# Attention stages of a two-layer backbone: end of the gate chain and its transposes issued behind the mLSTM key and query projections, convolution mean as a later step

## The chip, the core and the metric

The kernel runs on one core of a Trainium2 chip. The engines of a core work side by side and meet at semaphores: TensorE (PE) multiplies matrices, VectorE (DVE) and ScalarE (ACT) work element by element, GpSimd (POOL) does simple element-wise work, and SyncE (SP) issues the DMA transfers in the order of its own queue. The metric is the device time of one execution in microseconds (us), lower is better.

## The reference, cut to what matters

Two layers over 512 tokens of width 1024 (256 context tokens, 256 latent tokens; layer 1 needs the latent ones alone as outputs). Each layer has an attention stage and an expert stage:

```python
u  = adaLN_rmsnorm(x)                  # scale and shift come from c @ ada_w
a, q, k, v, o, gates, dq, dk, dv = split(u @ in_w)
# 1. conv module: gated input, depthwise convolution over 31 taps, layernorm, silu
y  = silu(layernorm(depthwise_conv31(a1 * sigmoid(a2)) + conv_b))
# 2. bidirectional mLSTM, 4 heads of 64: input and forget gates per head and direction
F  = cumsum(log_sigmoid(fgate));  M = running_max(igate - F)
w  = exp(igate - F - M) * (q @ k.T)    # masked on one side per direction
h1 = (w @ v) / max(|sum(w)|, exp(-(F + M)))
# 3. differential attention, 4 heads, rotary positions
h2 = (softmax(q1 @ k1.T) - lam * softmax(q2 @ k2.T)) @ dv
x += gate * (concat(y, h1, h2) @ out_w)
x += gate * peer_experts(adaLN_rmsnorm(x))   # product keys, 16384 experts
```

## The kernel before

The kernel is one program, written once in a natural order. A scheduler sets each engine's instruction order from that program and from a model of the work; where two instructions meet in one buffer, a semaphore makes the later one wait. Buffers are tiles of a pool with a **tag**: tiles with one tag share the tag's slots, and a new tile waits until the slot's former tile has been read for the last time.

An attention stage (`front`) runs as follows, at 50 to 345 us of the span in layer 0 and 2057 to 2300 us in layer 1:

- **Projections.** `proj` and `projv` read weights of 512 KB each on SP's queue; ACT writes the high part of each weight (`whi`), POOL the rest (`wlo`), and PE makes 24 matmuls for each projection (lines 319 to 321, three products per weight block; `projv` lines 350 to 352). The order in the program is: gate rows and conv inputs (`projg`, lines 333 to 335), second conv input, mLSTM output gates (MO0, MO1), mLSTM keys (MK0, MK1), queries (MQ0, MQ1), values, and then the steps of the string `ORDER`.
- **Gate chain.** `gate_rows` works on tiles of 64 rows x 512 tokens (heads and directions in rows): from line 520 to line 561 some 40 small operations of DVE with a few of ACT between them, scans included (lines 547 and 551). Its last part takes an exp, writes `rows` (line 565), and turns the chain's columns with eight transposes on PE (line 571) into `ah` and `ea`, which the heads need.
- **Convolution.** `conv` makes 62 multiply-adds on DVE (2 blocks x 31 taps, line 491 for 60 of them), then the layernorm: a mean by two matmuls on PE (line 495), line 497, squares, an rsqrt, lines 503 and 504, and a sigmoid on ACT (line 507).
- **mLSTM heads.** For each head PE spreads `rows` (line 613), ACT and DVE write the decay matrix E (lines 621, 625, 627), PE multiplies queries by keys (line 634), DVE multiplies that into E (line 639), and PE makes E times values (line 645).
- **Late modulation, layer 0 only.** `late` computes three of the six adaLN vectors. Its weights come as 12 tiles `w` of 1 MB, which use the slots of tags `kT` and `qT` in turn. PE multiplies half the columns of a tile (line 216) and DVE the other half (lines 147 and 149, four operations a tile), into an accumulator tile of tag `PT`, which has two slots.

The string `ORDER` is 'kmcvkk0k123' before: k is one pair of rotary keys and queries, m the mLSTM heads, c the whole convolution, v the values, digits are heads of differential attention.

Of the kernel before, what the change touches and what calls it, by code (L numbers as in the profile page):

```python
# [7 lines left out]
F32 = mybir.dt.float32  # L8
# [4 lines left out]
AF = mybir.ActivationFunctionType  # L13
# [22 lines left out]
LO = ('p', 'p')  # L36
ORDER = ('kmcvkk0k123', 'kmcvkk0k123')
NSUM = 4
# [11 lines left out]
class Net:  # L50
# [317 lines left out]
    def front(self, l, P, c0, late):  # L368
# [17 lines left out]
        first = self.projg(I["w_first"][l, 0], h, 0, ("f", "f", "f", "d"))  # L386
        rows = self.gate_rows(P, first[0], K)

# [6 lines left out]
        og = K["og"] = F.tile([128, 2, n], F32, name="og")  # L395
        v = K["v"] = F.tile([128, 4, 512], F32, name="v", tag="v")
        up = F.tile([128, 2, ns, T + 30], F32, name="up")
# [17 lines left out]
        for b in range(2):  # L415
            nc.scalar.activation(mq[:, b], self.proj(W[BLK_MQ + b], h, c0), AF.Copy)
        for k, p in enumerate(self.projv(I["w_v"][l, 0], h)):
            pv = p.rearrange("p t (a b e) -> p t a b e", b=2, e=64)
            for tt in range(2):
                for b in range(2):  # L420
                    nc.scalar.activation(vx[:, 2 * k + tt, b::2, 64 * b:64 * b + 64], pv[:, tt, :, b, :], AF.Copy)
# [11 lines left out]

        def values():
            for k in range(2):
                for t2, p in enumerate(self.projv(I["w_v"][l, 1 + k], h)):
                    nc.scalar.activation(v[:, 2 * t2:2 * t2 + 2, 256 * k:256 * k + 256], p, AF.Copy)
# [3 lines left out]
        for s in ORDER[l]:  # L441
            if s == "m":
                self.mlstm(P, K, rows, c0)
            elif s == "c":
                cy = self.conv(P, up, n)
            elif s == "v":
                values()
            elif s == "k":
                keys(seen)
                seen += 1  # L450
            else:
                self.diff(P, K, int(s), c0)
# [30 lines left out]
    def conv(self, P, up, n):  # L483
        nc = self.nc
        ys = [self.frontp.tile([128, n], F32, name=f"cy{b}") for b in range(2)]
        for b in range(2):
# [3 lines left out]
            for k in range(1, CONV_K):  # L490
                nc.vector.scalar_tensor_tensor(y, up[:, b, :, k:k + T], P["conv_w"][:, b, k:k + 1], y,  # L491
                                         op0=OP.mult, op1=OP.add)
        mu = self.ps("a")[:, :n]
        for b in range(2):
            nc.tensor.matmul(mu, self.ones, ys[b], start=b == 0, stop=b == 1)
        for b in range(2):
# [12 lines left out]
        self.log_exp(last)  # L509
        return ys  # L510

    def gate_rows(self, P, ps, K):

        nc, F = self.nc, self.frontp
        T1 = F.tile([128, 4, TT], F32, name="gr1", tag="v")
        T2 = F.tile([64, 4, TT], F32, name="gr2", tag="vx")
        G = T1[:, 0]
        Fg, e, u = (T1[0:64, k] for k in (1, 2, 3))
        r, L, Bl, M = (T2[:, k] for k in range(4))
        nc.vector.tensor_scalar(G, ps, P["gate_b"][:, 0:1], None, op0=OP.add)  # L520
# [11 lines left out]
        nc.vector.scalar_tensor_tensor(L, Fg, 0.0, L, op0=OP.min, op1=OP.subtract)  # L532
        lh, ll, ih, il = e, u, r, Fg

# [26 lines left out]
        nc.vector.tensor_add(out[:, 1], out[:, 1], Bl)  # L561
        nc.scalar.activation(out[:, 1], out[:, 1], AF.Exp, scale=-1.0)
        rows = F.tile([128, 2, TT], F32R, name="rows")
# [5 lines left out]
        for k, src in enumerate((ih, il)):  # L569
            for tt in range(4):  # L570
                nc.tensor.transpose(pt[:, (4 * k + tt) * 64:(4 * k + tt) * 64 + 64],
                                    src[:, tt * 128:(tt + 1) * 128], self.ident[:64, :64])
        pv = pt.rearrange("p (k t r) -> p k t r", k=2, t=4)
# [612 lines left out]
```

## Time and profile before

| quantity | before |
|---|---|
| time, median of 3 runs | 3119.13 us (3117.34 to 3130.06) |
| the profiled execution: time, span | 3119.87 us, 3118.2 us |
| TensorE's granted clock over the span | 0.973 of full speed |
| PE busy | 2933.3 us, 94% of the span |
| DVE busy | 2233.9 us, 72% |
| ACT, POOL busy | 1440.0 us, 1378.2 us |

Busy times are shares of the whole span, while the change touches two stretches of some 290 and 240 us. What bounds those has to be read from windows of the trace, from the list of waits and from the timeline of each engine in them.

### The profile page before, as it was taken

How to read it: one execution, taken by the hardware profiler on the slowest of the kernel's cores; microseconds unless marked ns; L12 is line 12 of the kernel's file. 1: busy time of each engine (PE TensorE's matmuls, PEld its weight loads, DVE VectorE, ACT ScalarE, POOL GpSimd, SP SyncE). 2: the span in 40 equal slices, each digit the busy share in tenths (PEclk: the TensorE clock that was granted, in tenths of full speed). 3: DMA queues.
4: the chain of work that ended last, by engine and by line, in shares of the span. 5: the costliest groups of instructions: out<-in, count | busy, mean ns of one | idle time of the engine just before them, and what ended most of it. 6: DMA issues, size and time to landing. Idle time of an engine off the chain costs nothing.

```text
span 3118.2 us, 43562 instructions
## 1 busy us (share of the span) xinstructions
PE 2933.3 (94%) x14930; PEld 2424.5 (78%) x14930; DVE 2233.9 (72%) x4604; ACT 1440.0 (46%) x2861; POOL 1378.2 (44%) x1079
## 2 busy tenths in 40 slices
PE   7899989999999978989999999978989998999998
PEld 4476578888888856767888888867689998788887
DVE  7987637867777769998555545486759789666665
ACT  4345443346666632223333333345455765555554
POOL 4434245656666645343434334163478875000000
PEclk9999999999999989999999999989999999999999
DMA  6511124345655577776555555121255876987874
GB/s 225 176 48 55 39 82 137 123 146 182 209 207 208 208 237 254 239 239 213 174 174 169 179 154 180 41 87 51 67 172 170 274 257 234 314 267 256 260 229 136
DMA packets 249806, 550.95 MB, mean 177 GB/s; under 512 B 17440, under 2 KB 118304, under 8 KB 246384
## 3 DMA queue, kind: packets, MB, share of 16 engines
q1 hardware_dynamic: 248864, 545.74, 53.3%
q8 instruction: 118, 1.93, 0.3%
q0 software_dynamic: 720, 2.43, 0.2%
q14 instruction: 104, 0.85, 0.1%
HBM read 456.87 MB, written 91.23 MB: 176 GB/s over the span
## 4 chain that ended last, share of the span: by engine, by line
PE 64%; DVE 13%; DMA 5%; issue 2%; ACT 1%; POOL 1%; SPq 0%; DVEq 0%; ACTq 0%; POOLq 0%
PE h L887 9%; PE h L888 9%; PE h L889 9%; PE acc L1000 6%; PE acc L999 5%; PE acc L1001 5%; PE f L836 3%; DVE wtr L196 3%; PE f L999 3%; PE f L1000 3%; PE f L1001 3%; DMA ga<-act 1%; DMA v<-in_peer_v 1%; DVE cy L491 1%; DMA u<-in_peer_u 1%
## 5 line engine op out<-in xcount | busy, mean ns | idle before, releaser
L870 POOL TENSOR_TENSOR ul<-u,uh 128x512 fp32r<-128x512 f32 x448 | 594.8, 1339 | 382.9 <-ACT uh L869 370.5
L887 PE MATMUL h<-hh,uh 128*128 128x512 f32 (+1 forms) x2048 | 694.4, 339 | 3.2 <-DVE rt_stg L838 2.1
L889 PE MATMUL h<-hh,ul 128*128 128x512 f32 (+1 forms) x2048 | 691.2, 338 | 5.1 <-POOL ul L870 5.1
L888 PE MATMUL h<-hl,uh 128*128 128x512 f32 (+1 forms) x2048 | 691.5, 338 | 0.0
L869 ACT ACTIVATE vh<-v 128x512 fp32r<-128x512 f32 x512 | 319.5, 628 | 590.1 <-PE acc L1001 368.3
L869 ACT ACTIVATE uh<-u 128x512 fp32r<-128x512 f32 x512 | 318.4, 628 | 468.2 <-PE h L888 320.8
L870 POOL TENSOR_TENSOR vl<-v,vh 128x512 fp32r<-128x512 f32 x208 | 303.3, 1470 | 366.5 <-ACT vh L869 357.3
L889 PEld LDWEIGHTS h<-hh,ul 128*128 128x128 f32 x2048 | 391.0, 191 | 46.7 <-POOL ul L870 5.8
L887 PEld LDWEIGHTS h<-hh,uh 128*128 128x128 f32 x2048 | 391.3, 191 | 45.4 <-DVE rt_stg L838 2.7
L888 PEld LDWEIGHTS h<-hl,uh 128*128 128x128 f32 x2048 | 391.4, 191 | 38.0
L1000 PE MATMUL acc<-vl,wh 128*128 128x512 f32 x1024 | 402.5, 393 | 4.3 <-DVE vl L870 4.1
L999 PE MATMUL acc<-vh,wh 128*128 128x512 f32 x1024 | 401.6, 392 | 1.5 <-ACT vh L869 1.5
L1001 PE MATMUL acc<-vh,wl 128*128 128x512 f32 x1024 | 400.6, 391 | 0.0
L241 POOL TENSOR_TENSOR wlo<-wt,whi 128x512 fp32r<-128x512 f32 x164 | 248.1, 1524 | 246.4 <-ACT whi L240 224.5
L838 DVE TENSOR_REDUCE rt_stg<-f 128x256 f32<-128x512 f32 x384 | 243.6, 687 | 137.4 <-PE f L836 136.6
L965 DVE TENSOR_TENSOR ga<-ga,g 128x512 f32<-128x512 f32 x192 | 163.2, 856 | 177.4 <-DMA ga<-act 99.6
L870 DVE TENSOR_TENSOR vl<-v,vh 128x512 fp32r<-128x512 f32 x304 | 205.6, 693 | 107.4 <-ACT vh L869 107.1
L999 PE MATMUL f<-vh,wh 128*128 128x512 f32 x512 | 205.1, 401 | 44.8 <-DVE accS L1007 34.3
L1000 PEld LDWEIGHTS acc<-vl,wh 128*128 128x128 f32 x1024 | 193.7, 189 | 49.2 <-DVE vl L870 9.2
L1007 DVE TENSOR_TENSOR accS<-accS,f 128x512 f32<-128x512 f32 x252 | 171.3, 680 | 83.0 <-PE f L1001 82.9
L999 PEld LDWEIGHTS acc<-vh,wh 128*128 128x128 f32 x1024 | 193.9, 189 | 42.5 <-ACT vh L869 2.2
L1001 PEld LDWEIGHTS acc<-vh,wl 128*128 128x128 f32 x1024 | 193.6, 189 | 40.2
(320 smaller groups left out, 5372.1 us busy)
## 6 DMA issues: line engine op xcount, KB each, us to landing
u<-in_peer_u SPq DMA_DIRECT2D x256, 512.0 KB, 4.1
v<-in_peer_v SPq DMA_DIRECT2D x256, 512.0 KB, 4.4
G<-rt_stg SPq DMA_DIRECT2D x24, 2048.0 KB, 7.0
act<-ga SPq DMA_DIRECT2D x152, 256.0 KB, 3.4
ga<-act SPq DMA_DIRECT2D x152, 256.0 KB, 4.2
g<-G SPq DMA_DIRECT2D x32, 1024.0 KB, 6.2
wa<-in_ada_t SPq DMA_DIRECT2D x56, 512.0 KB, 4.2
w<-in_ada_w SPq DMA_DIRECT2D x20, 1024.0 KB, 6.4
```

The source lines that it names most:

```text
L241: nc.gpsimd.tensor_sub(lo, raw, hi)
L838: nc.vector.tensor_reduce(stg[:, :, t4 + k2:t4 + k2 + 2].rearrange("p j t -> p t j"), pg.rearrange("p (t x j) -> p t j x", t=2, x=2), axis ...
L869: nc.scalar.activation(hi, raw[:, k * 512:(k + 1) * 512], AF.Copy)
L870: lo_eng.tensor_sub(lo, raw[:, k * 512:(k + 1) * 512], hi)
L887: nc.tensor.matmul(o, uh, hh[:, c, c0:], start=c == 0, stop=False)
L888: nc.tensor.matmul(o, uh, hl[:, c, c0:], start=False, stop=False)
L889: nc.tensor.matmul(o, ul, hh[:, c, c0:], start=False, stop=c == NB - 1)
L965: nc.vector.tensor_mul(av, av, g)
L999: nc.tensor.matmul(A, wh[:, t], vh, start=s0 and jj == 0, stop=False)
L1000: nc.tensor.matmul(A, wh[:, t], vl, start=False, stop=False)
L1001: nc.tensor.matmul(A, wl[:, t], vh, start=False, stop=s1 and jj == 1)
L1007: nc.vector.tensor_add(o, o, A)
```

## The change

Three things change, in both layers. First, `gate_rows` ends at line 561, and its last part (exp, `rows`, transposes, `ah`, `ea`) becomes `gate_cols`, called behind the key and query projections; its exp and its transposes are held in program order. Second, buffers: the four temporary rows that were one tile of tag `vx` are now two tiles `gr2` and `gr3` of tag `PT`, and the tiles `v` and `vx` get their slots in other places. Third, `conv` ends with the taps, and the layernorm with sigmoid becomes a step n that stands behind the values in `ORDER`; its two mean matmuls are held in program order.

```diff
@@ -34,7 +34,7 @@
 LAG = (16, 4)
 HB = 4
 LO = ('p', 'p')
-ORDER = ('kmcvkk0k123', 'kmcvkk0k123')
+ORDER = ('kmcvnkk0k123', 'kmcvnkk0k123')
 NSUM = 4
 MORE = (4, 6)
 WB = 5
@@ -384,7 +384,7 @@
         W = I["w_t"][l]
         K = self.K = {}
         first = self.projg(I["w_first"][l, 0], h, 0, ("f", "f", "f", "d"))
-        rows = self.gate_rows(P, first[0], K)
+        gates = self.gate_rows(P, first[0], K)
 
         vx = K["vx"] = F.tile([128, 4, 4, 128], F32, name="vx", tag="vx")
         for hh in range(4):
@@ -393,7 +393,6 @@
         km = K["km"] = F.tile([128, 2, TT], F32, name="km", tag="km")
         mq = K["mq"] = F.tile([128, 2, n], F32, name="mq", tag="mq")
         og = K["og"] = F.tile([128, 2, n], F32, name="og")
-        v = K["v"] = F.tile([128, 4, 512], F32, name="v", tag="v")
         up = F.tile([128, 2, ns, T + 30], F32, name="up")
         nc.gpsimd.memset(up[:, :, :, 0:15], 0.0)
         nc.gpsimd.memset(up[:, :, :, T + 15:T + 30], 0.0)
@@ -414,6 +413,7 @@
             nc.scalar.activation(km[:, b], self.proj(W[BLK_MK + b], h, 0), AF.Copy, scale=0.125)
         for b in range(2):
             nc.scalar.activation(mq[:, b], self.proj(W[BLK_MQ + b], h, c0), AF.Copy)
+        rows = self.gate_cols(K, *gates)
         for k, p in enumerate(self.projv(I["w_v"][l, 0], h)):
             pv = p.rearrange("p t (a b e) -> p t a b e", b=2, e=64)
             for tt in range(2):
@@ -432,6 +432,7 @@
             self.rot(pq[:, T - c0:TT - c0], qT[:, b, T - c0:], 0.125)
 
         def values():
+            v = K["v"] = F.tile([128, 4, 512], F32, name="v", tag="v")
             for k in range(2):
                 for t2, p in enumerate(self.projv(I["w_v"][l, 1 + k], h)):
                     nc.scalar.activation(v[:, 2 * t2:2 * t2 + 2, 256 * k:256 * k + 256], p, AF.Copy)
@@ -443,6 +444,8 @@
                 self.mlstm(P, K, rows, c0)
             elif s == "c":
                 cy = self.conv(P, up, n)
+            elif s == "n":
+                self.conv_norm(P, up, n, cy)
             elif s == "v":
                 values()
             elif s == "k":
@@ -490,9 +493,13 @@
             for k in range(1, CONV_K):
                 nc.vector.scalar_tensor_tensor(y, up[:, b, :, k:k + T], P["conv_w"][:, b, k:k + 1], y,
                                          op0=OP.mult, op1=OP.add)
+        return ys
+
+    def conv_norm(self, P, up, n, ys):
+        nc = self.nc
         mu = self.ps("a")[:, :n]
         for b in range(2):
-            nc.tensor.matmul(mu, self.ones, ys[b], start=b == 0, stop=b == 1)
+            self.tc.keep_in_program_order(nc.tensor.matmul(mu, self.ones, ys[b], start=b == 0, stop=b == 1))
         for b in range(2):
             nc.vector.scalar_tensor_tensor(ys[b], mu, -1.0 / 256.0, ys[b], op0=OP.mult, op1=OP.add)
         split = lambda t: t.rearrange("p (s t) -> p s t", t=T)
@@ -507,16 +514,15 @@
             last = nc.scalar.activation(sg, ys[b], AF.Sigmoid)
             nc.vector.tensor_mul(ys[b], ys[b], sg)
         self.log_exp(last)
-        return ys
 
     def gate_rows(self, P, ps, K):
 
         nc, F = self.nc, self.frontp
         T1 = F.tile([128, 4, TT], F32, name="gr1", tag="v")
-        T2 = F.tile([64, 4, TT], F32, name="gr2", tag="vx")
+        T2, T3 = (F.tile([64, 2, TT], F32, name=k, tag="PT", bufs=2) for k in ("gr2", "gr3"))
         G = T1[:, 0]
         Fg, e, u = (T1[0:64, k] for k in (1, 2, 3))
-        r, L, Bl, M = (T2[:, k] for k in range(4))
+        r, L, Bl, M = T2[:, 0], T2[:, 1], T3[:, 0], T3[:, 1]
         nc.vector.tensor_scalar(G, ps, P["gate_b"][:, 0:1], None, op0=OP.add)
         nc.vector.tensor_copy(Fg, G[64:128])
         ig = G[0:64]
@@ -530,7 +536,7 @@
         nc.vector.tensor_mul(r, r, u)
         nc.vector.tensor_add(L, L, r)
         nc.vector.scalar_tensor_tensor(L, Fg, 0.0, L, op0=OP.min, op1=OP.subtract)
-        lh, ll, ih, il = e, u, r, Fg
+        lh, ll, ih, il = e, u, Fg, ig
 
         def split(hi, lo, v):
             nc.vector.tensor_scalar(hi, v, SPLIT, None, op0=OP.add)
@@ -559,7 +565,12 @@
         nc.vector.tensor_scalar(out[:, 0], M, -1.0, None, op0=OP.mult)
         nc.vector.tensor_add(out[:, 1], Bh, M)
         nc.vector.tensor_add(out[:, 1], out[:, 1], Bl)
-        nc.scalar.activation(out[:, 1], out[:, 1], AF.Exp, scale=-1.0)
+        return out, ih, il
+
+    def gate_cols(self, K, out, ih, il):
+
+        nc, F, keep = self.nc, self.frontp, self.tc.keep_in_program_order
+        keep(nc.scalar.activation(out[:, 1], out[:, 1], AF.Exp, scale=-1.0))
         rows = F.tile([128, 2, TT], F32R, name="rows")
         nc.scalar.activation(rows[:64], out, AF.Copy)
         nc.vector.tensor_sub(rows[64:], out, rows[:64])
@@ -568,8 +579,8 @@
         pt = self.ps("m")
         for k, src in enumerate((ih, il)):
             for tt in range(4):
-                nc.tensor.transpose(pt[:, (4 * k + tt) * 64:(4 * k + tt) * 64 + 64],
-                                    src[:, tt * 128:(tt + 1) * 128], self.ident[:64, :64])
+                keep(nc.tensor.transpose(pt[:, (4 * k + tt) * 64:(4 * k + tt) * 64 + 64],
+                                         src[:, tt * 128:(tt + 1) * 128], self.ident[:64, :64]))
         pv = pt.rearrange("p (k t r) -> p k t r", k=2, t=4)
         nc.vector.tensor_copy(K["ah"], pv[:, 0])
         nc.scalar.activation(K["ea"], pv[:, 1], AF.Exp)
```

How this moves instructions, at three places. Line numbers of the changed kernel are larger from `conv` on: its lines 502, 526, 567, 582, 624, 632, 636, 638, 645 and 494 are lines 495, 520, 561, 571, 613, 621, 625, 627, 634 and 491 of before.

**First place, layer 0 between MO1 and the key projections.** On PE before, the first two tiles `w` of the late modulation alternate with the transposes, ahead of the first key matmul:

```order
L216 MATMUL a<-w_745,cc 2x512 x2
L571 MATMUL m<-ident,gr_567 128x64 x4
L216 MATMUL a<-w_753,cc 2x512 x2
L571 MATMUL m<-ident,gr_566 128x64 x4
L319 MATMUL f<-hh,whi 128x512
L320 MATMUL f<-hl,whi 128x512
```

After the change, the two tiles stand together and the key matmuls follow at once:

```order
L216 MATMUL a<-w_728,cc 2x512 x2
L216 MATMUL a<-w_736,cc 2x512 x2
L319 MATMUL f<-hh,whi 128x512
L320 MATMUL f<-hl,whi 128x512
L321 MATMUL f<-hh,wlo 128x512
```

The third tile, w_744, then comes behind all 48 key matmuls of MK0 and MK1, and w_752 seven matmuls later:

```order
L321 MATMUL f<-hh,wlo 128x512
L319 MATMUL f<-hh,whi 128x512
L320 MATMUL f<-hl,whi 128x512
L321 MATMUL f<-hh,wlo 128x512
L216 MATMUL a<-w_744,cc 2x512 x2
L319 MATMUL f<-hh,whi 128x512
L320 MATMUL f<-hl,whi 128x512
L321 MATMUL f<-hh,wlo 128x512
```

So MK0 and MK1 no longer stand behind the transposes, and the third tile stands behind them; the eight transposes follow some 55 rows further on, behind MQ1 and eight tiles of `w`. On DVE before, the first two tiles' eight operations stand ahead of the gate chain's first one (line 520):

```order
L147 TENSOR_SCALAR ada<-w_745,cc 128x512
L307 TENSOR_TENSOR hl<-nm,hh 128x256
L149 SCALAR_TENSOR_TENSOR ada<-w_745,cc,ada 128x512 x2
L149 SCALAR_TENSOR_TENSOR ada<-w_753,cc,ada 128x512 x4
L520 TENSOR_SCALAR gr_566<-f,small_112 128x512
L521 COPY gr_566<-gr_566 64x512
```

On DVE after the change, they stand behind the gate chain's last one (line 567), and those of w_744 behind four taps more:

```order
L566 TENSOR_TENSOR gr_566<-gr_567,gr_568 64x512
L494 SCALAR_TENSOR_TENSOR cy_1606<-up,small_112,cy_1606 128x512
L567 TENSOR_TENSOR gr_566<-gr_566,gr_568 64x512
L147 TENSOR_SCALAR ada<-w_728,cc 128x512 x2
L149 SCALAR_TENSOR_TENSOR ada<-w_728,cc,ada 128x512 x2
L149 SCALAR_TENSOR_TENSOR ada<-w_736,cc,ada 128x512 x4
L494 SCALAR_TENSOR_TENSOR cy_1606<-up,small_112,cy_1606 128x512
L494 SCALAR_TENSOR_TENSOR cy_1607<-up,small_112,cy_1607 128x512
L494 SCALAR_TENSOR_TENSOR cy_1606<-up,small_112,cy_1606 128x512
L494 SCALAR_TENSOR_TENSOR cy_1607<-up,small_112,cy_1607 128x512
L149 SCALAR_TENSOR_TENSOR ada<-w_744,cc,ada 128x512 x4
```

The reason is the tag: `gr2` and `gr3` hold both slots of `PT` until line 567, and the accumulator that lines 147 and 149 write needs one.

**Second place, layer 1 ahead of the first head.** On PE before, the last matmuls of DK0 are followed by the heads' first two, then the convolution mean, then the rotation of the keys and the query projection DQ0:

```order
L320 MATMUL f<-hl,whi 128x512
L321 MATMUL f<-hh,wlo 128x512
L613 MATMUL m<-rows,sel 128x256 x2
L495 MATMUL a<-cy_18866,ones 128x256
L495 MATMUL a<-cy_18867,ones 128x256
L361 MATMUL f<-rp_t,perm 128x256
L319 MATMUL f<-hh,whi 128x256
L320 MATMUL f<-hl,whi 128x256
```

On PE after the change, the mean is gone from there (it stands behind the last head) and the rotation and DQ0 follow at once:

```order
L320 MATMUL f<-hl,whi 128x512
L321 MATMUL f<-hh,wlo 128x512
L624 MATMUL m<-rows,sel 128x256 x2
L361 MATMUL f<-rp_t,perm 128x256
L319 MATMUL f<-hh,whi 128x256
L320 MATMUL f<-hl,whi 128x256
L321 MATMUL f<-hh,wlo 128x256
L319 MATMUL f<-hh,whi 128x256
```

On DVE all 62 taps of layer 1 stand ahead of the first operation on E in both kernels.

**Third place, layer 0 at the step of the convolution's sigmoid.** On ACT before, the sigmoids (sg) stand between values and weights, with one table load ahead and one behind:

```order
L648 ACTIVATE ml_dab<-m 64x512
L649 ACTIVATE ml_nu<-m 64x512
L507 ACT_TABLE_LOAD
L507 ACTIVATE sg<-cy_1606 128x512
L240 ACTIVATE whi<-wt 128x512 x3
L437 ACTIVATE v<-f 128x2x256
L240 ACTIVATE whi<-wt 128x512
L507 ACTIVATE sg<-cy_1607 128x512
L248 ACT_TABLE_LOAD
```

On ACT after the change, they stand within the decay matrices E of the last mLSTM head, and each change between sigmoid and exp has a table load:

```order
L632 ACTIVATE E<-m,ah 128x384
L514 ACT_TABLE_LOAD
L514 ACTIVATE sg<-cy_1606 128x512
L638 ACT_TABLE_LOAD
L638 ACTIVATE E<-E 128x128
L632 ACTIVATE E<-m,ah 128x256 x2
L514 ACT_TABLE_LOAD
L514 ACTIVATE sg<-cy_1607 128x512
L638 ACT_TABLE_LOAD
L638 ACTIVATE E<-E 128x128
```

With one more load behind the last of these rows, two loads have become five.

## Rows read from the trace of the kernel before

**Rows 1.** The page: the chain that ended last, and DMA issues of `w`.

```profile
PE 64%; DVE 13%; DMA 5%; issue 2%; ACT 1%; POOL 1%; SPq 0%; DVEq 0%; ACTq 0%; POOLq 0%
...
w<-in_ada_w SPq DMA_DIRECT2D x20, 1024.0 KB, 6.4
```

**Rows 2.** Waits of PE, 0 to 310 us: total, times, longest.

```profile
PE m L571 <- DVE gr L555: 6.4, 1, 6.4
```

**Rows 3.** Waits of PE, 2000 to 2400 us.

```profile
PE m L571 <- DVE gr L555: 11.3, 1, 11.3
PE a L495 <- DVE cy L491: 6.7, 1, 6.7
```

**Rows 4.** Windows, layer 1: busy PE, PEld, DVE, ACT, POOL; clock, DMA share, GB/s.

```profile
2060.00:2090.00 30.00, 18.67 (x109) 16.00 (x109) 29.52 (x38) 14.26 (x20) 13.61 (x9) 0.80 0.28 86
2090.00:2120.00 30.00, 28.26 (x188) 25.53 (x186) 29.63 (x49) 10.41 (x24) 19.64 (x13) 0.97 0.22 72
```

**Rows 5.** Timeline of layer 1, DVE and PE: start, us, instruction, idle before.

```profile
2057.52 0.75 DVE L520 TENSOR_SCALAR gr<-f,small 128x512 f32<-128x512 f32 x1 [8.17 <-PE f L335]
...
2098.14 27.89 DVE L491 SCALAR_TENSOR_TENSOR cy<-up,small,cy 128x256 f32<-128x256 f32 x43
2127.35 0.76 DVE L497 SCALAR_TENSOR_TENSOR cy<-a,cy 128x256 f32<-128x256 f32 x2 [1.31 <-PE a L495]
2128.20 0.43 DVE L363 TENSOR_TENSOR rp_u<-f,rope 128x256 f32<-128x256 f32 x1
...
2129.36 0.60 DVE L625 TENSOR_SCALAR E<-m,ah 128x128 f32<-128x128 f32 x2
...
2131.54 0.70 PE L634 MATMUL m<-mq,km 64*128 64x256 f32 x2
```

**Rows 6.** Timeline of layer 0, DVE.

```profile
68.58 7.16 DVE L149 SCALAR_TENSOR_TENSOR ada<-w,cc,ada 128x512 f32<-128x512 f32 x6
75.67 0.74 DVE L520 TENSOR_SCALAR gr<-f,small 128x512 f32<-128x512 f32 x1
...
109.92 0.67 DVE L561 TENSOR_TENSOR gr<-gr,gr 64x512 f32<-64x512 f32 x1
110.53 2.06 DVE L149 SCALAR_TENSOR_TENSOR ada<-w,cc,ada 128x512 f32<-128x512 f32 x3
```

**Rows 7.** Timeline of layer 0, PE.

```profile
71.96 0.39 PE L335 MATMUL f<-hh,wlo 128*128 128x512 f32 x1
...
76.55 0.47 PE L319 MATMUL f<-hh,whi 128*128 128x512 f32 x1 [2.16 <-DVE gr L520]
...
94.70 1.88 PE L216 MATMUL a<-w,cc 128*2 128x512 f32 x4
103.02 0.69 PE L571 MATMUL m<-ident,gr 64*128 64x64 f32 x4 [6.44 <-DVE gr L555]
103.63 3.57 PE L216 MATMUL a<-w,cc 128*2 128x512 f32 x4
107.14 0.69 PE L571 MATMUL m<-ident,gr 64*128 64x64 f32 x4
...
175.97 1.02 PE L495 MATMUL a<-cy,ones 128*128 128x512 f32 x2
...
186.67 1.12 PE L634 MATMUL m<-mq,km 64*128 64x512 f32 x2
```

**Rows 8.** Windows, layer 0: columns as in rows 4.

```profile
84.40:94.60 10.20, 10.20 (x46) 8.26 (x44) 10.20 (x16) 5.98 (x8) 8.97 (x3) 1.00 0.19 52
107.75:186.67 78.92, 73.81 (x324) 46.09 (x323) 75.81 (x111) 20.88 (x49) 34.80 (x23) 0.97 0.50 167
```

**Rows 9.** Timeline of SP's queue: the late tiles `w` from the third to the last.

```profile
99.44 8.17 SPq L210 DMA_DIRECT2D w<-in_ada_w  x2
...
139.47 7.20 SPq L210 DMA_DIRECT2D w<-in_ada_w  x2
```

**Rows 10.** Table loads on ACT around the sigmoid, layer 1.

```profile
2142.76 1.28 ACT L507 ACT_TABLE_LOAD   x1
2144.06 0.42 ACT L507 ACTIVATE sg<-cy 128x256 f32<-128x256 f32 x1
```

**Rows 11.** Groups of DVE by line, 200 to 232 us: count, busy, mean ns.

```profile
L503 DVE TENSOR_TENSOR cy<-cy,up 128x512 f32<-128x512 f32 x2 | 1.3, 688 | 0.0
L504 DVE TENSOR_SCALAR cy<-cy,small 128x512 f32<-128x512 f32 x2 | 1.0, 540 | 0.0
```

## The prediction, put on record before the changed kernel ran

> **What bounds the kernel now.** I began with the chain that ended last: 64% of it is TensorE (PE) and 13% VectorE (DVE) [rows 1]. PE decides most of the span, so the change is worth what it takes from PE's waits in the two attention stages. The list of PE's waits names those it can touch. In layer 0 the transposes wait 6.4 us for DVE's gate chain [rows 2]. In layer 1 they wait 11.3 us, and the convolution mean waits 6.7 us for the taps [rows 3]. That is 24.4 us, 0.8% of the time, the most that the list promises. (About 0.5%, 15.6 us, is what a measurement of this kernel can tell from no change.)
>
> The next question is whether DVE, for which PE waits, has room. In layer 1 it has none: it is busy 29.52 and 29.63 us of two windows of 30 us [rows 4]. The timeline shows the same stretch as one unbroken piece of DVE work: line 520 starts at 2057.52, the last 43 taps start at 2098.14 and take 27.89, so they end at 2126.03, 68.5 us later, and only then come line 497 and the first operations on E [rows 5]. So in layer 1 PE's waits are the shadow of a DVE that is full. In layer 0 the gate chain runs from 75.67 to 110.53, 34.9 us [rows 6]. PE waits 2.16 us for its first operation and 6.44 us at the transposes, and the first head's matmul (line 634) comes at 186.67 [rows 7]. From 107.75 to there PE is busy 73.81 of 78.92 us and DVE 75.81 [rows 8]: both are nearly full.
>
> **Layer 0, up to the first head.** Three things are removed. The eight operations of the first two late tiles leave the front of line 520. The gate projection's last matmul ends at 71.96 + 0.39 = 72.35 [rows 7], so the gate chain can start at about 72.4, 3.3 us earlier, and PE's wait of 2.16 goes. The wait of 6.44 at the transposes goes. With it goes a slow stretch: four matmuls on a tile w take 1.88 us ahead of that wait and 3.57 behind it [rows 7], 1.7 more, which is the clock's lower level (1.2 instead of 2.4 GHz).
>
> One wait is added. Both slots of PT are held by gr2 and gr3, so DVE's work on the first two tiles w comes behind the gate chain, and until it is done the slots of kT and qT hold those tiles, and the third tile's transfer can't start. The gate chain now ends at 72.4 + 34.9 = 107.3. The first tile's four operations, at 2.06 / 3 = 0.69 us each [rows 6], end at 110.0. A tile takes 6.4 us to land [rows 1]: 116.4. PE comes to its first tile at 94.70 - 2.2 = 92.5, spends 3.8 us on two of them, and 48 key matmuls at 10.2 / 46 = 0.22 us each [rows 8] last until about 107. So I expect a new wait of 9 to 10 us, at line 216, for a DMA. It replaces the 6.44 and brings its own slow clock, for which I take the same 1.7. What stands behind it on PE is everything up to the heads.
>
> From 116.4 PE has the work that it had from 107.75 on (73.81), less the 48 matmuls (10.6) and the mean (1.0), plus the transposes (1.4) and the slow clock (1.7): 65.3, so the first head would come at 181.7. DVE has from line 520 on the same operations as before up to there: taken with all its idle time, 111.0 us, that gives 183.4, and without the 3.1 idle us of [rows 8] 180.3. I take 182, **a gain of 4.7 us** (3.3 to 6.4).
>
> The late tiles are on SP's queue behind value weights that stood behind them before. Ten tiles, from the third to the last, were issued from 99.44 to 139.47 + 7.20 = 146.67 [rows 9], 10.5 us for a pair. Behind the change they start at 110.0, and PE needs the last one about 70 matmuls (15 us) ahead of the first head, so at 167: five pairs in 57 us, 11.4 for a pair. One transfer and eight operations in a row are 6.4 + 5.5 = 11.9. That is close, and is a rival below. The earlier memsets of vx on POOL cost nothing: POOL is busy 34.80 of 78.92 us there [rows 8]; without that cover, they would delay the low parts of weights.
>
> **Layer 0, the convolution's layernorm.** The same operations now stand behind the third head's, and the sigmoids fall among the exps of the fourth. Three more table loads cost 1.28 us each [rows 10], 3.8 us; two halves of lines 503 and 504 (1.3 and 1.0 us [rows 11]) stand on DVE ahead of the sigmoid on which ACT's exps now queue up. If PE had other work all the while, the cost would be nothing; if all of it is on the path, 6.1. By the order, PE has five projection matmuls, about 1 us, ahead of the head's first product and little behind, so I take **a loss of 5**.
>
> The Trainium skill has a rule against such an order (ScalarE: Activation LUTs, section "What ACT_TABLE_LOAD costs"): a switch to another set costs the load of about 1.28 us and a drain of about 1.38 us, and so one should batch by set. By that, three more switches would cost 8.0 us and the forecast would be 4 us higher. The trace agrees on the load alone: it starts at 2142.76, ends at 2144.04, and the sigmoid starts at 2144.06 [rows 10], with no drain between.
>
> **Layer 1.** Both waits (18.0 us) go from their places. But DVE's operations from line 520 to the last tap are the same, it has no idle time to give, and line 520 itself waits for the projection as before [rows 5]. The taps end again at about 2126.0, and all 62 stand ahead of the first operation on E. PE now runs ahead, through DQ0, and stops at the first head's product, which needs a PSUM buffer that the operations on E free. From line 363 to the end of the third such operation it took 2129.96 - 2128.20 = 1.76 us [rows 5], so the first product comes at 2127.8 instead of 2131.54: 3.7 us earlier, since line 497 and DQ0 no longer stand between. PE's wait there is 2127.8 less 2131.54 - 18.0 = 2113.5, some 14 us: **the waits move, they don't go.** Against it stands the layernorm, now between the heads and the attention: fourteen operations of 0.38 us [rows 5] are at most 5.3 us, at the least nothing, since rotary keys and queries give PE work; most of it should be covered, and I take 1.2. Net **a gain of 2.5** (-1.6 to 3.7).
>
> **Sum.** 4.7 - 5 + 2.5 = 2.2 us less than the profiled execution's 3119.87: 3117.7. The median of the runs is 0.7 lower, so I forecast **3117**. With the bounds added up, it lies between 10.1 us less (3109) and 4.4 us more (3124).
>
> **Rivals.**
> - *The waits go.* If DVE finished its chain and taps earlier because PE and the weights no longer stop, all of 24.4 + 2.2 + 1.7 = 28.3 us would be gained: 3091. For it speaks only that some of DVE's operations are slowed in places; against it, that DVE is full in both stretches. 0.10.
> - *The late tiles decide, slower.* Each pair of tiles waits for DVE, and DVE's operations on them stand among taps. If a pair takes 15 us instead of 11.4, the last tile comes at 185 and the first head at 200, 13 us later than before; with the loss of 5 and the gain of 2.5 that is 3135. It decides from 11.4 us for a pair on. For it speaks the 11.9 above; against it, that both slots are in flight together. 0.14.
> - *Nothing comes of it.* The layer 1 wait moves in full, since more weights pass through POOL beside the taps and slow them, and the layernorm's place costs what the first heads gain: 3119 to 3124. 0.16.
> - *Forecast.* 0.60, with 3109 to 3124 as its own range.
>
> The range must leave out no more than 2 in 10: all of the first rival and about half of the second, so 3104 to 3132. Faster by over 0.5% is the first rival and a little of the forecast's edge, 0.12; slower by over 0.5% most of the second, 0.12; the rest, 0.76, is within 0.5%.
>
> **What the profile after would show.** If I am right: no wait of PE at the transposes (line 582) or the mean (502); in layer 0 a wait of 9 to 10 us at line 216 for a DMA near 107 to 116 us; in layer 1 some 14 us of wait at the first line 645 for DVE's line 636; from line 526 to the last tap still 68 to 69 us; five table loads in the fourth head of layer 0. I am wrong if the taps of layer 1 end several us earlier than 68 us behind line 526, if the first head of layer 0 starts before 178 or after 190, or if the fourth head of layer 0 shows no new wait of PE.

## The result and the profile after

The changed kernel takes 3151.11 us (median of 4 runs, 3149.61 to 3157.47) and the kernel before, on the same chips, 3118.24 (3113.99 to 3130.06): a ratio of 1.0103, 95% interval 1.0072 to 1.0134. I forecast 3117 in 3104 to 3132; it came out slower, and outside the range. The profiled span is 3149.9 us, 31.7 more than before. The page: span, busy times, and the granted clock in 40 slices.

```profile
span 3149.9 us, 43560 instructions
...
PE 2952.1 (94%) x14930; PEld 2438.4 (77%) x14930; DVE 2230.1 (71%) x4604; ACT 1440.6 (46%) x2861; POOL 1373.5 (44%) x1079
...
PEclk9898899999999989999999999988999999999999
```

PE is busy 18.8 us longer than before for the same 14930 matmuls, at a mean clock of 0.963 instead of 0.973; slices 2, 4, 5 and 28 show 8 where before shows 9. The rest of the 31.7 us is idle time. PE's waits say where (0 to 340 us, then 2050 to 2450 us; total, times, longest):

```profile
PE a L216 <- DMA w<-in_ada_w: 30.1, 2, 15.1
PE m L645 <- DVE E L636: 8.5, 2, 7.5
PE a L226 <- DVE red L160: 5.7, 3, 4.3
...
PE m L645 <- DVE E L636: 5.7, 1, 5.7
PE m L582 <- DVE gr L561: 5.5, 1, 5.5
...
PE m L582 <- DVE gr L562: 1.9, 1, 1.9
```

The wait at layer 0's transposes [rows 2] and the one at layer 1's mean [rows 3] have gone. Others stand for them: a second wait of 15 us for a late tile (the first of the two, in the first 15.1 us of the span, was there before), 5.7 us at line 226 of the late modulation, and waits at a head's first product of queries and keys (line 645, formerly 634). At layer 1's transposes (582, formerly 571) 7.4 of the 11.3 us are left. On PE's timeline the new ones of layer 0 and layer 1 are these (start, us, instruction, idle before):

```profile
119.00 3.57 PE L216 MATMUL a<-w,cc 128*2 128x512 f32 x4 [15.01 <-DMA w<-in_ada_w]
...
262.51 2.04 PE L645 MATMUL m<-mq,km 64*128 64x512 f32 x2 [7.48 <-DVE E L636]
...
2150.74 2.44 PE L645 MATMUL m<-mq,km 64*128 64x256 f32 x4 [5.69 <-DVE E L636]
```

I read the loss place by place. In layer 0 the first head's product of queries and keys comes at 192.9 instead of 186.7. By the third head's product of E and values PE has caught up (247.3, before 248.0), having put projections off. The fourth comes 25.7 us later, before 15.5: 10.2 lost. The attention heads behind it lose 12 more, and layer 1's gate chain starts 22.5 us late (2080.1, before 2057.5). Layer 1 loses 9 us, all of it in attention.

Two things in these places are not what I had reckoned with. The gate chain, 34.9 us before, takes 40.7 us in layer 0 and 39.8 in layer 1. The windows of both chains, with DVE's 28 operations on the tiles gr alone (us, DVE busy, clock, DMA share, GB/s): before,

```profile
75.67:110.59 34.92, 21.68 (x28) 0.85 0.34 111
2057.52:2092.45 34.93, 24.38 (x28) 0.80 0.25 76
```

and after,

```profile
71.05:111.77 40.72, 25.95 (x28) 0.94 0.21 67
2080.05:2119.81 39.76, 30.39 (x28) 0.89 0.34 106
```

The same 28 operations take 4.3 and 6.0 us longer. The longer chain is not yet a loss, though. In layer 1 the taps behind it win the time back: 60 of them (line 491, after the change 494) take 34.48 us instead of 39.43, and from the chain's start to the last tap it is 69.37 us instead of 68.51 (windows as above, DVE's busy time on the taps alone; before, then after):

```profile
2057.52:2126.03 68.51, 39.43 (x60) 0.87 0.27 84
2080.05:2149.42 69.37, 34.48 (x60) 0.87 0.27 84
```

In layer 0 DVE is busy only 3.1 us longer between the chain's start and the first head's product, but idle for 11.3 us there instead of 3.6 (all of DVE's operations; before, then after):

```profile
75.67:186.67 111.00, 107.42 (x150) 0.94 0.44 147
71.05:192.86 121.81, 110.51 (x152) 0.90 0.39 135
```

Most of that idle time is waits for the late tiles behind the chain, 7.4 us against 1.3 before (waits of DVE there: two lines of after, one of before):

```profile
DVE ada L147 <- DMA w<-in_ada_w: 4.5, 1, 4.5
DVE ada L149 <- DMA w<-in_ada_w: 2.9, 3, 2.4
...
DVE ada L149 <- DMA w<-in_ada_w: 1.3, 2, 0.9
```

The tile of the longest one was issued at 148.93, behind a weight on SP's queue that had waited 9.9 us for POOL's subtraction on the slot's former weight (waits of SP, 125 to 160 us):

```profile
SPq L234 <- POOL wlo L241: 12.7, 2, 9.9
```

The second thing is in the fourth head of layer 0, where five table loads stand on ACT in 10.6 us (timeline of ACT):

```profile
253.63 1.28 ACT L514 ACT_TABLE_LOAD   x1
254.93 0.63 ACT L514 ACTIVATE sg<-cy 128x512 f32<-128x512 f32 x1
255.57 1.28 ACT L638 ACT_TABLE_LOAD   x1
...
257.92 1.28 ACT L514 ACT_TABLE_LOAD   x1
...
259.86 1.28 ACT L638 ACT_TABLE_LOAD   x1
...
262.96 1.28 ACT L248 ACT_TABLE_LOAD   x1
...
264.92 0.37 ACT L427 ACTIVATE kT<-f 128x256 f32<-128x256 f32 x1
...
265.65 0.63 ACT L240 ACTIVATE whi<-wt 128x512 fp32r<-128x512 f32 x1
```

Behind them in ACT's queue stand not only the head's exps, but the copy that frees a PSUM buffer of rotary keys (line 427) and the next weight's high part (line 240). PE's next projection comes at 269.0, behind both. That PE had none to go on with for want of these two is my reading.

### The profile page after: what moved, and what is told of

Same layout as the page of the kernel before. It is cut to its first block, busy times and chain, and to the rows that moved or that the text cites. A ratio compares the mean times of both kernels' runs of the same rounds, so it can differ in the third digit from the quotient of the medians.

```text
span 3149.9 us, 43560 instructions
## 1 busy us (share of the span) xinstructions
PE 2952.1 (94%) x14930; PEld 2438.4 (77%) x14930; DVE 2230.1 (71%) x4604; ACT 1440.6 (46%) x2861; POOL 1373.5 (44%) x1079
## 4 chain that ended last, share of the span: by engine, by line
PE 67%; DVE 12%; DMA 4%; issue 2%; ACT 1%; POOL 1%; SPq 0%; DVEq 0%; POOLq 0%; ACTq 0%
PE h L898 10%; PE h L899 10%; PE h L900 10%; PE acc L1011 6%; PE acc L1010 6%; PE acc L1012 6%; DVE wtr L196 3%; PE f L1010 3%; PE f L847 3%; PE f L1011 3%; PE f L1012 3%; DMA ga<-act 1%; PE f L333 1%; PE f L334 1%; DVE cy L494 1%
## 5 line engine op out<-in xcount | busy, mean ns | idle before, releaser
L241 POOL TENSOR_TENSOR wlo<-wt,whi 128x512 fp32r<-128x512 f32 x164 | 240.6, 1478 | 270.9 <-ACT whi L240 266.3
```

The costliest lines, as they stand in the source:

```text
L241: nc.gpsimd.tensor_sub(lo, raw, hi)
```

## The experiments

Theory N: the layernorm's place in layer 0 is the larger part, through ACT's queue, and the gate part the smaller, through the chain that grows. Rivals: the gate part is the larger, or its loss comes from the two slots of PT. All ratios are to the kernel before, with 95% intervals.

**Each part alone.** `e1_gates` makes the gate part alone (gate_cols late, gr2 and gr3 in PT), `e2_norm` the layernorm alone (the last two lines).

```diff
-        T2 = F.tile([64, 4, TT], F32, name="gr2", tag="vx")
+        T2, T3 = (F.tile([64, 2, TT], F32, name=k, tag="PT", bufs=2) for k in ("gr2", "gr3"))
...
+        rows = self.gate_cols(K, *gates)
...
-ORDER = ('kmcvkk0k123', 'kmcvkk0k123')
+ORDER = ('kmcvnkk0k123', 'kmcvnkk0k123')
```

> The gate part alone (late end of the gate chain, gr2 and gr3 on tag PT, v in values); the convolution is whole as before. Before is 3118.2 us, the full change 3151.1. Theory N (the layernorm as a later step costs most: in the traces the fourth head of layer 0 loses 10 us, the differential attention 12.5 us in layer 0 and 10 in layer 1): 3117 to 3124 us, since only the first head of layer 0 comes late (2.8 us by the traces) and layer 1 gains nothing while the mean still waits for the taps. Rival G (the gate part costs most, because the tiles of the late modulation wait for PT and every projection behind them shifts): 3138 us or more.

> The convolution's layernorm as step n alone; gate chain and buffers as before. Theory N: 3143 to 3150 us, and in the trace the first attention product of layer 1 stands 10 us behind the last mLSTM head's matmuls instead of 5, with the fourth head of layer 0 waiting 7 to 9 us. Rival G: 3115 to 3125 us.

Gates: 3125.07 us, 1.0024 (1.0015 to 1.0033). Layernorm: 3138.74, 1.0070 (1.0056 to 1.0084). So the layernorm is the larger part, some 22 us, and the gates some 7. Each is just outside the range that theory N gave, and far from rival G.

**The gate part's slots.** `e3_gates_vx` and `e4_all_vx` are e1 and the whole change with the temporary rows in one tile of tag vx again, so that PT's slots stay free.

```diff
-        T2, T3 = (F.tile([64, 2, TT], F32, name=k, tag="PT", bufs=2) for k in ("gr2", "gr3"))
+        T2 = F.tile([64, 4, TT], F32, name="gr2", tag="vx")
```

> The gate part alone with its four temporary rows in one tile of tag vx as before, so that PT is free for the late modulation. If the slots of PT cause the 15 us wait for a tile w in layer 0: that wait is below 3 us here, and the run is 4 to 9 us faster than the gate part on PT, 3110 to 3118 us. Rival (DVE is full there and decides, wherever PE waits): within 3 us of the gate part on PT.

> The full change with the four temporary rows on tag vx as before. Theory N: 3141 to 3148 us, still over 20 us slower than before, since the layernorm's place is untouched. Rival G by the slots of PT: 3116 to 3126 us.

3129.36, 1.0033 (1.0020 to 1.0046), and 3149.67, 1.0097 (1.0079 to 1.0115). Freeing the slots buys nothing. In layer 0 the longest wait for a tile falls from e1's 14.6 us to 5.1 (I had expected under 3), but PE now waits for DVE at line 158, in the late modulation too (waits of PE in e3, 40 to 340 us):

```profile
PE a L158 <- DVE ada L149: 10.2, 2, 9.6
PE a L216 <- DMA w<-in_ada_w: 6.1, 3, 5.1
```

The chain there takes 36.7 us, and still the first head's product comes at 192.5 (before 186.7, e1 194.1). So the chain's growth alone does not make it late. In e3's layer 1 PE has a new wait, and POOL has one ahead of it:

```profile
PE f L351 <- POOL wlo L241: 11.1, 1, 11.1
...
POOL vx L392 <- DVE gr L562: 12.2, 1, 12.2
```

POOL's memset of vx (line 392) waits for gr2's slot, and the low parts of weights stand behind it on POOL.

**The layernorm by layer.** `e5_norm_l1` is e2 in layer 1 alone; in layer 0 step n stands right behind c, which is the old place.

```diff
-ORDER = ('kmcvkk0k123', 'kmcvkk0k123')
+ORDER = ('kmcnvkk0k123', 'kmcvnkk0k123')
```

> The layernorm as a later step in layer 1 alone; layer 0, gate chain and buffers as before. The traces of the layernorm alone in both layers showed layer 0 losing 14 us up to the end of its attention and layer 1 3 us. If that holds for the median: 3119 to 3123 us, 1 to 5 above before. Rival (most of its 21 us comes from layer 1): 3128 us or more.

3125.15, 1.0002 (0.9990 to 1.0015). Nearly all of the layernorm's 22 us belong to layer 0.

**Table loads.** `e6_norm_exp` is e2 with a sigmoid that needs no other table; `e11_exp` puts the same sigmoid into the kernel before.

```diff
-            last = nc.scalar.activation(sg, ys[b], AF.Sigmoid)
+            nc.scalar.activation(sg, ys[b], AF.Exp, scale=-1.0)
+            nc.vector.tensor_scalar(sg, sg, 1.0, None, op0=OP.add)
+            nc.vector.reciprocal(sg, sg)
```

> The layernorm as a later step in both layers, its sigmoid computed as 1 / (1 + exp(-y)) with an exp on ACT and an add and a reciprocal on DVE, so that no table load is left around it. If the three more loads make the fourth head of layer 0 late: that head's distance from the third falls from 24.6 us by 4 to 8, and the run is at 3131 to 3135 us instead of 3138.7. Rival (the head waits for the layernorm's chain of DVE work, loads or not): 3138 us or more, the distance within 2 us of 24.6.

> Before, with the convolution's sigmoid as 1 / (1 + exp(-y)): seven table loads fewer. If loads cost what they stand in front of on ACT, before has little to gain, since its sigmoids stand where PE has other work: 3114 to 3119 us against 3118, ratio 0.998 to 1.001. Rival (each load costs wherever it stands): 9 us or more faster, ratio below 0.997.

3129.13, 1.0024 (1.0013 to 1.0035): of the layernorm's loss 4.6 thousandths, 14 us, are gone. In the kernel before the same edit gains nothing and may cost a little: 3127.50, 1.0017 (1.0003 to 1.0031). The fourth head is only 1.9 us shorter than e2's, which is the sign that I had given for the rival; but PE does other work in it. Windows from the third head's product of E and values to the fourth's, all engines (us, PE, PEld, DVE, ACT, POOL; clock, DMA share, GB/s): e2,

```profile
242.30:266.90 24.60, 16.58 (x51) 9.19 (x51) 13.89 (x31) 17.13 (x35) 4.24 (x10) 0.79 0.02 9
```

and e6:

```profile
243.50:266.20 22.70, 22.52 (x89) 15.12 (x89) 19.66 (x33) 11.68 (x31) 9.06 (x14) 1.00 0.11 38
```

51 matmuls at a clock of 0.79, against 89 at 1.00. What isn't done here is done in the attention, and there it shows: from the fourth head's product to the last attention head's product with values, layer 0 takes 109.2 us in e2 and 97.7 in e6 (before 99.0).

**DVE as the bound of layer 1.** `e7_taps` puts 30 taps of layer 1 behind the second head's first operations on E, and the layernorm behind the first attention head; `e8_taps_gates` adds the late gates in layer 1; `e12_best` is e8 with the sigmoid of e6; `e13_gates_l1` is the late gates of layer 1 alone.

```diff
+                with self.tc.issue_after(self.tri) if n == T and b == 1 else ExitStack():
                     nc.vector.scalar_tensor_tensor(y, up[:, b, :, k:k + T], P["conv_w"][:, b, k:k + 1], y,
...
+ORDER = ('kmcnvkk0k123', 'kmcvkk0nk123')
```

> Layer 1 alone: the 30 multiply-adds of the convolution's second block are queued on DVE behind the second head's first operations on E, and the layernorm behind the first attention head; gate chain as before. Theory (DVE's work ahead of the first head bounds layer 1, so moved waits can gain nothing, but moved DVE work can): the first product of E and values comes at 66 to 72 us behind the gate chain's start instead of 79, and the run is at 3108 to 3114 us. Rival (the waits are not DVE's doing, or all is given back by heads and attention): 3116 us or more.

> As the run with the 30 taps moved, and the late end of the gate chain with it, in layer 1 alone (layer 0 as before). By the theory the two go together: with DVE relieved, PE no longer stops for the transposes and the first product of E and values comes 60 to 66 us behind the gate chain's start: 3102 to 3109 us. Rival (the gates' place gives nothing even then): within 2 us of the run with the taps alone.

> What helped, together: in layer 1 the late end of the gate chain, 30 taps behind the second head's first operations on E, and the layernorm behind the first attention head; in both layers the sigmoid from exp; layer 0 otherwise as before. The runs with taps and gates gave 0.9983: with the loads gone too, 0.995 to 0.998. Rival (the gains of the parts are given back by the attention's clock): 0.998 to 1.001.

> The late end of the gate chain in layer 1 alone (rows on tag PT there), layer 0 as before. Theory (the gate part's 7 us are layer 0's: the late modulation's tiles and what stands behind them): ratio 0.998 to 1.001 to before, and the gate chain of layer 1 takes 39 to 40 us instead of 34.9, as in the full change. Rival (layer 1's longer chain costs it): 1.002 or more.

e7: 3120.96, 0.9995 (0.9984 to 1.0006). e8: 3118.17, 0.9983 (0.9973 to 0.9993). e12: 3132.99, 1.0034 (1.0022 to 1.0047). e13: 3123.52, 1.0009 (0.9997 to 1.0021). In e7 the first head's product of E and values comes 69.8 us behind the chain's start instead of 79.1. So DVE does bound that place, but nearly all of the 9 us is given back later. In e8 it comes after 70.2 us, not the 60 to 66 expected: the late gates add nothing there. In e13 layer 1's chain takes 39.8 us, as expected, and yet the first product of queries and keys comes 74.1 us behind its start, as before (74.0).

e12 is a plain miss: with the other sigmoid it is 5 thousandths slower than e8. So that edit, which also adds two operations of DVE for each block, can cost more than the loads that it saves. What costs there was not found, and e6's 14 us are the worth of the whole edit where the sigmoids stand among a head's exps, not a clean price of the loads.

**The low parts.** What lengthens the chain? A weight's low part is a subtraction on POOL (line 241), and it runs more often beside the chain once PE doesn't stop. `e9_lo_act` is the kernel before with ACT writing a plain copy there (it leaves out the subtraction), `e10_gates_lo_act` the same on e1.

```diff
-            nc.gpsimd.tensor_sub(lo, raw, hi)
+            nc.scalar.activation(lo, raw, AF.Copy)
```

> Before, with the low part of every attention-stage weight written by ACT as a plain copy of the weight instead of POOL's subtraction (the output is not the reference's; PE, DVE and DMA do what they did). Theory (POOL's work beside the gate chain slows DVE's operations): the gate chain's own operations take 17 to 20 us in both layers, instead of 22.1 and 24.8. Rival (they are slow by themselves or by their waits): within 1 us of 22.1 and 24.8.

> The gate part alone (rows on tag PT), with the same low parts by ACT (the output is not the reference's). With the low parts on POOL the gate chain's own operations had grown from 22.1 to 26.1 us in layer 0 and from 24.8 to 29.5 in layer 1. Theory: here they are within 1 us of the run before with low parts by ACT, and the chain from its first to its last operation is no longer than there. Rival (PE running on, or DMA, slows them): still 4 us longer than there.

3052.89, 0.9775 (0.9758 to 0.9791), and 3058.70, 0.9802 (0.9783 to 0.9822). The 28 operations of e9, in the windows of both chains, columns as in those of before:

```profile
69.89:100.64 30.75, 18.02 (x28) 0.89 0.41 125
2021.18:2049.26 28.08, 18.01 (x28) 1.00 0.32 94
```

18.0 us in both layers, against 21.7 and 24.4 before and 26.0 and 30.4 after: POOL's subtractions lengthen the chain, the more of them the more (7, 11, 13 and 15 stand in those four windows). In e10 the 28 operations take 18.0 us too, and the chain 31.0 and 28.0 us, about as in e9. The first head's product of layer 0 comes 1.7 us later than in e9 (170.8, 169.1), where e1's came 7.4 us later than before's. So most of that lateness goes with the subtractions. Yet the gate part still costs 5.8 us in all, against 7 with them: the longer chain is shown, but it is not what the gate part costs in the end. I find 4.3 of the 5.8 in the third head of layer 0 (36.1 us from the second head's product of E and values, e9 31.8), and there e10's timeline of ACT shows why:

```profile
215.59 1.28 ACT L508 ACT_TABLE_LOAD   x1
...
217.54 1.28 ACT L633 ACT_TABLE_LOAD   x1
...
219.78 1.28 ACT L508 ACT_TABLE_LOAD   x1
...
221.72 1.28 ACT L633 ACT_TABLE_LOAD   x1
...
224.36 1.28 ACT L248 ACT_TABLE_LOAD   x1
```

Late gates push taps back, and with them the sigmoids, into a head's exps, with no layernorm moved. e1 has the same five loads in its third head (36.7 us, before 33.0). No kernel tests this by itself. e3 has late gates too, but only two loads there and 34.2 us in that head, and it is no faster than e1; it has waits of its own, so that settles nothing.

**A better place for the low parts.** `e14_lo_dve` is the kernel before with the same subtraction on DVE, `e15_lo_half` with every second one there, `e16_all_lo_dve` the whole change with all of them there, and `e17_lo_dve_taps` e14 with layer 1 as in e8.

```diff
-            nc.gpsimd.tensor_sub(lo, raw, hi)
+            nc.vector.tensor_sub(lo, raw, hi)
```

> Before, with the low part of every attention-stage weight subtracted by DVE instead of POOL (the reference's arithmetic). With the low parts off POOL and DVE both, the kernel was 69 us faster. A subtraction of this size takes 0.69 us on DVE; 164 of them are 113 us of DVE work, of which the stretch ahead of layer 1's first head has some 25 (17 us). Theory (POOL beside DVE costs DVE more than the same work on DVE): 20 to 50 us faster than before, ratio 0.984 to 0.994. Rival (DVE is full there, so its own work costs as much as the slowing): 0.997 to 1.01.

> As the run with the low parts on DVE, but with only every second one there, the others on POOL. Theory: half of that run's gain, within 5 us. Rival (a mixed load is best, since neither engine is the bound): more than that run's gain.

> The full change, with the low parts on DVE instead of POOL. Theory: the chain's growth is gone, so this is at most 20 us slower than before with the low parts on DVE (33 with them on POOL), the rest being the layernorm's table loads and layer 0's late modulation. Rival: 30 us or more slower than that run.

> Low parts on DVE, and in layer 1 the late end of the gate chain, the 30 taps behind the second head's first operations on E and the layernorm behind the first attention head. Theory (DVE still bounds layer 1's first head, now with the low parts in its queue): 3 to 9 us faster than the low parts on DVE alone, 3070 to 3076 us. Rival (given back later in heads and attention, where DVE now has the low parts too): within 2 us of 3079 or slower.

e14: **3079.11 us, 0.9853 (0.9829 to 0.9877), faster than both kernels.** e15: 3100.11, 0.9934 (0.9916 to 0.9953), somewhat under half of it. e17: 3082.00, 0.9870 (0.9848 to 0.9892), no better than e14, as its rival had it. The page of e14 shows that DVE, 164 operations richer, is busy only 17 us longer than before (2233.9), and POOL 243 less (1378.2). The 164 at 0.69 us are 113 us, so DVE's other operations take some 96 us less. The second row is the wait at the transposes in its layer 1, 11.3 before [rows 3]:

```profile
PE 2926.3 (95%) x14930; PEld 2418.0 (79%) x14930; DVE 2251.1 (73%) x4768; ACT 1440.3 (47%) x2861; POOL 1135.2 (37%) x915
...
PE m L571 <- DVE gr L555: 3.7, 1, 3.7
```

e16: 3091.02, 0.9909 (0.9885 to 0.9934). On this footing the change costs 12 us instead of 33. Two things are gone at once, though: the chain's growth (29.8 us in layer 0, e14 29.6), and the loads among the exps, since here the sigmoids fall behind the fourth head (timeline of ACT, two loads):

```profile
270.73 1.28 ACT L514 ACT_TABLE_LOAD   x1
272.02 0.63 ACT L514 ACTIVATE sg<-cy 128x512 f32<-128x512 f32 x1
274.43 0.63 ACT L514 ACTIVATE sg<-cy 128x512 f32<-128x512 f32 x1 [1.78 <-DVE cy L515]
275.08 1.28 ACT L248 ACT_TABLE_LOAD   x1
```

Its fourth head takes 17.3 us (e14 18.0, after 25.7). How the 21 us divide between the two, these runs don't tell.

## Why the prediction was wrong

- **"A loss of 5" for layer 0's layernorm: the step that failed, by its size.** The place and the five loads were as forecast, and so was a wait of PE in the fourth head (7.5 us at line 645). But the bound of 6.1 counted loads and halves on the way to the exps, and took PE's other work as given. Its inputs come through the same queue of ACT, as high parts and PSUM copies: 51 matmuls in the fourth head's stretch of e2, 89 in e6. The step costs some 21 us (e2 less e5), and 14 of it go with the sigmoid that needs no load (e6).
  I had weighed a rule of the Trainium skill (ScalarE: Activation LUTs, section "What ACT_TABLE_LOAD costs"): an estimate by its figure is 8.0 us for three more switches, which is nearer and still short. The trace again shows no drain between load and sigmoid (253.63 + 1.28 = 254.91, then 254.93).
- **"The gate chain now ends at 72.4 + 34.9": wrong.** It started at 71.05, and took 40.7. I had carried over a duration measured while PE stood still and fewer weights came through (7 subtractions beside the chain, now 13). The wait at line 216, forecast at 9 to 10 us, is 15.0: the tile came 2.6 us later than forecast, and PE reached it at 104.0, 3 us earlier. The first head's product comes 6.2 us later than before instead of 4.7 earlier. That POOL's subtractions lengthen the chain is shown by e9, e10 and e14, and that most of the lateness goes with them by e10. But the longer chain is only part of the way there: DVE's work up to that product grew by 3.1 us, and its idle time by 7.7.
- **The late tiles as the bound** (the slower rival) came true in part. PE's list shows no further long wait for a tile. But DVE waits 7.4 us for late tiles, 6.1 more than before, and PE's 4.3 us at line 226 are for an operation of DVE that stands behind the longest of these waits. The size was not the rival's: PE comes to the last two tiles at 167.1 and 170.6, where I needed 167 and the rival had 185.
- **Layer 1.** "The waits move, they don't go" was right: the first product comes 70.7 us behind the chain's start instead of 74.0, 3.3 earlier, forecast 3.7. From the chain's start to the last tap it took 69.4 us, forecast 68 to 69. The wait at the product is 5.7 instead of 14, because 7.4 stayed at the transposes, again by the longer chain; I had forecast none there. The net gain of 2.5 was not there: e5 and e13 together come to 1.0011.
- **The sum.** Gates 1.0024 and layernorm 1.0070 make 1.0094 of the measured 1.0103. Layer 0's two terms, -4.7 and +5, came out as losses of about 5 (e1 less e13) and 21 us.

Open is part of the loss in layer 1's attention (9 us in the profiled execution). The same 281 matmuls took 60.2 us in e13, as before, and 67.0 in e1 (columns as in [rows 4]):

```profile
2182.20:2242.40 60.20, 55.34 (x281) 39.11 (x280) 43.70 (x88) 33.05 (x79) 27.32 (x26) 1.00 0.20 62
```

```profile
2195.50:2262.50 67.00, 63.11 (x281) 42.80 (x280) 42.71 (x88) 32.58 (x78) 27.17 (x26) 0.87 0.18 56
```

In the changed kernel that clock was 0.90. In the four other runs with the layernorm behind layer 1's heads and in front of the attention (e2, e4, e5, e6) it is 0.92 to 0.95 from the fourth head's product to the attention's last product of keys and queries, and that stretch takes 68 to 69 us, against 59.5 at 1.00 before; they reach it earlier, though, and e5 as a whole is no slower than before. Whether the change causes the lower clock there, or it differs from execution to execution, wasn't settled.

## What to carry to other kernels

A stall that is removed sets its engine's suppliers going too: before carrying a chain's duration over, look at what else will run beside it, here POOL beside DVE, and then add up the whole stretch, since the slowing can only have moved. Read the waits of the engine that your engine waits for, too: DVE's late tiles don't show in PE's list. When an operation is moved on an in-order queue, cost it by everything that stands behind it there, weights and buffer copies for other engines included, not by the chain you are looking at. Where an engine is full, also look at who slows it: 164 subtractions moved onto the fuller engine gained 1.5%.

## What the runs showed of the hardware

Operations of DVE take longer beside POOL's subtractions. On the timeline of after, an operation of 64x512 elements takes 1.76 us in the midst of the chain and 0.68 at its end:

```profile
88.53 1.76 DVE L538 SCALAR_TENSOR_TENSOR gr<-gr,gr 64x512 f32<-64x512 f32 x1
...
111.09 0.68 DVE L567 TENSOR_TENSOR gr<-gr,gr 64x512 f32<-64x512 f32 x1
```

In before the operation of line 538 (there 532) takes 0.67. With POOL's subtractions gone, the 28 operations take 18.0 us in every chain of e9 and e14. On POOL a subtraction takes 1.30 us (median of after; the longest 8.51), on DVE 0.69 (median of e14).

The Trainium skill (SBUF — State Buffer, section "SBUF: two separate sides") has VectorE and GpSimd share a pair of ports that one holds for a whole instruction while the other waits, where the VectorE operation is in a two-port mode, or has two SBUF inputs and the GpSimd one reads SBUF. The traces agree in that both sides are stretched; no run here looked at the ports themselves. They also show operations that are not stretched: in after, 12 of line 636, which read a PSUM buffer, ran wholly beside a subtraction and took at most 0.35 us, as they do alone, while eight taps of 128x512 that ran so took 1.10 us at the median and up to 1.78, alone 0.74.
